# One transformer layer on one core: all q, k and v projected in a stage of their own before attention

## The chip, the cores and the metric

The kernel runs on one core of one Trainium2 chip. The metric is device time in microseconds for one execution of the whole layer; three runs of the kernel before gave a median of 2404.73 us (2404.29 to 2406.45). The engines are named as in the profile: PE is TensorE, DVE is VectorE, ACT is ScalarE, POOL is GpSimd, SP is SyncE, which here only issues DMAs.

## The reference

The sequence has 2048 tokens of width 1024, 16 heads of 64, and a feed-forward width of 2816. DEPTH is 1, so only layer 0 runs, and its mixer is the chunked softmax attention with a relative-position bias.

```python
def rms_norm(x, g):
    y = xf * lax.rsqrt(jnp.mean(xf * xf, axis=-1, keepdims=True) + RMS_EPS)
    return (y * g).astype(x.dtype)

def chunk_relpos_attention(h, w_qkv, w_o, rel_bias):      # CHUNK = 64, LEFT_CHUNKS = 8
    q, k, v = split_heads(h, w_qkv)
    for c in range(n_chunks):                             # chunk c reads chunks c-8 .. c
        sc = einsum(q_blk, k[:, :, k0:k1]) * scale + bias
        p = softmax(sc)
        outs.append(einsum(p, v[:, :, k0:k1]))
    return merge_heads(o) @ w_o

def reference(...):
    h = rms_norm(x, g_pre_mix);  m = chunk_relpos_attention(h, w_qkv, w_o, rel_bias)
    x = x + rms_norm(m, g_post_mix)
    h = rms_norm(x, g_pre_ffn)
    x = x + rms_norm((silu(h @ w_gate) * (h @ w_up)) @ w_down, g_post_ffn)
```

## The kernel before, in words

**Layout and products.** Activations lie transposed: 128 features on the partitions, tokens along the free axis, 512 tokens ("half", in the changed kernel "quarter", tiles of 128x512) at a time. Every float32 operand of a dense product is cut into a rounded part `hi` and a remainder `lo` (ACT makes `hi`, DVE subtracts to get `lo`: `split`, `split_part`), and a product is three PE matmuls, hi·hi, hi·lo and lo·hi (`products`, lines 207 to 209).

**Order of the work.** The PE order is the order in which the code issues it; the order on the other engines is set by a list scheduler when the kernel is built. Two groups of 1024 tokens are worked on one after the other. In a group, the attention of 16 jobs (8 pairs of heads times 2 halves) is the frame, and a generator `dense()` gives out the q, k, v and output projections in small pieces that `fill(t)` puts between the attention's steps. One job has four slots, one for each 128 queries. A slot issues: `scores` (q·k for two heads into the PSUM tile `st`, of which there is one; then on DVE the bias and the running minimum, one operation per head, on ACT the exponential, on DVE a reciprocal of the row sum, on POOL the scaling), dense filler, `transposed` (PE transposes of an earlier slot's probabilities into one of two PSUM tiles `tt`, four key blocks of each head, which DVE copies for the first head and ACT for the second; after more filler, the fifth key block of both heads), and once in a job `output` (probabilities times v into `po`). A job of the first 512 tokens has no earlier keys, so its slots have 128, 256, 384 and 512 keys instead of 640, and no fifth block.

**The filler.** `qk_job` makes one pair's q and k for one half from eight feature blocks, 2·8 products; `v_job` makes v for four heads with two matmuls for each feature block, of 512 and 256 columns (lines 540 and 543). Where a tile has to be laid out anew across partitions (`stage` to `q` and `k`), a DMA does it. `o_half` is the output projection of a half. The feed-forward part after it, of gate and up (`gate_up`) and down (`down`), uses seven block products in place of eight (`BLOCKS`: B11, B21, T1, T2, B22, T3, T4), with sums of blocks of the activations (class `Blocks`: `first`, `second`, `third`) and of the weights (S1 to S4). The weight sums are made in DRAM by accumulating DMAs that POOL issues (`weight_sums`), in the slots of the attention.

**The step from attention to feed-forward.** In the last group both calls of `o_half` stand behind the attention's end; `blocks[0].first` and `blocks[0].second`, which load x1, normalise it, form the sums and split them, run beside the two of them (lines 1440 and 1442).

Of the kernel before, what the change touches and what calls it, by code (L numbers as in the profile page):

```python
# [26 lines left out]
NG = SEQ // GROUP  # L27
NF = DFF // P
# [13 lines left out]
REST = 52  # L42

# [4 lines left out]
C256 = 0.110  # L48
QK_COST = 2 * KT * 3 * C512
V_COST = 4 * KT * 3 * C256  # L50


@with_exitstack
def trunk(
# [4 lines left out]
    w_a: bass.AP,  # L59
# [34 lines left out]
    attn_d = [[dram.tile([P, HALF], F32, name=f"attn_{p}_{i}") for p in range(NPAIR)] for i in range(2 * NG)]  # L94
    khist_d = [[dram.tile([P, 2, HALF], F32, name=f"kh_{p}_{g}") for p in range(NPAIR)] for g in range(NG - 1)]
    vhist_d = [[dram.tile([P, 4, 256], F32, name=f"vh_{j}_{g}") for j in range(NPAIR // 2)] for g in range(NG - 1)]
# [3 lines left out]
    sum_gu = {n: dram.tile([NF // 2, P, 1024], F32, name=f"gu_{n}") for n in ("S1", "S2", "S3", "S4")}  # L100
# [6 lines left out]
    def bias_rows():  # L107
        ext = phase["ap"].tile([P, 6 * HALF], F32, tag="k", name="ext", bufs=2)[0:NH, 0:EXT]
# [9 lines left out]
    plan, roomy = [], set()  # L118
    for g in range(NG):
        plan += [w_a[n] for n in range(3 * NPAIR // 2)]  # L120
        plan += [w_o[c] for c in range(4)] * 2
        if g == 0:
            roomy |= set(range(len(plan) - 6, len(plan) + 2))
# [17 lines left out]
    def fetch():  # L141
# [4 lines left out]
        raw = None  # L146
        if n in roomy:

            raw = phase["ap"].tile([P, 4 * HALF], F32, tag="q", name=f"raw_{n}", bufs=2)
            sp.dma_start(raw, plan[n])  # L150
        for c in range(2):
            here = slice(c * 1024, c * 1024 + 1024)
            if n in roomy:
                part = raw[:, here]
            else:
                if "fp" in phase:
                    part = phase["fp"].tile([P, 1024], F32, tag="w4", name=f"raw_{n}_{c}", bufs=4)
                else:
                    part = wp.tile([P, 1024], F32, tag="raw", name=f"raw_{n}_{c}", bufs=2)
                sp.dma_start(part, plan[n][:, here])  # L160
            split_part(*tiles[c], part)
# [4 lines left out]
    class Slab:  # L166
# [15 lines left out]
        def both(self, k):  # L182

            n = (k % 4) * 256
            return self.tiles[k // 4].both[:, :, n : n + 256]

# [10 lines left out]
    def dense_bank(n, wide=False):  # L197

        if "psf" in phase and n % 2:
            return phase["psf"].tile([P, HALF], F32, tag="pd", name="mm", bufs=6)  # L200
        if wide and n % 2:
            return phase["psa"].tile([P, 4, P], F32, tag="tt", name="mm", bufs=2).rearrange("p a b -> p (a b)")
        return ps.tile([P, HALF], F32, tag="mm", name="mm")
# [44 lines left out]
    def scratch(name):  # L248
# [6 lines left out]
        return xp.tile([P, 640], F32, tag="sc", name=name, bufs=4)  # L255
# [104 lines left out]
    class Prep:  # L360


        def __init__(self, s, src, gain):
            self.s, self.src, self.gain = s, src, gain
            self.done = set()

        def buffer(self):
            t = xp.tile([P, 10 * HALF], F32, tag="big", name="prep", bufs=1)
            self.t = t.rearrange("p (k c) -> p k c", k=10)
            self.total, self.r = self.t[:, 8, :], self.t[:, 9, :]  # L370

        def load(self, w=1.6, lag=3):

            def one(k):
                def go():
                    if k == 0:
                        self.buffer()
                    if k < KT:
                        sp.dma_start(self.t[:, k, :], self.src[:, k, :])
# [341 lines left out]
    def gather(g, s):  # L721
# [5 lines left out]
        for _ in range(2):  # L727
            yield
# [975 lines left out]
```

## Time and profile before

| | |
|---|---|
| median of three runs | 2404.73 us |
| span of the profiled execution | 2403.1 us |
| PE / DVE / ACT / POOL busy | 99% / 63% / 43% / 12% of the span |
| granted TensorE clock | 0.998 of full speed |
| DMA | 488.36 MB, mean 203 GB/s |

The profiled execution has a span, from its first to its last instruction, of 2403.1 us, 1.6 us under the median of the runs; the page gives no other time for it. Busy is time in which an engine had an instruction in hand; matmuls overlap in the pipeline, so a mean duration of a matmul (389 ns for 512 columns) is longer than the distance between two of them.

### The profile page before, as it was taken

The numbers are of one execution on the slowest core, as the hardware profiler recorded it, in microseconds if no ns is written. First come the engines' busy times: TensorE is split into PE (matmuls) and PEld (weight loads), VectorE is DVE, ScalarE is ACT, GpSimd is POOL, SyncE is SP. The second block draws the span as 40 slices with busy tenths as digits, with TensorE's granted clock in tenths as the row PEclk, the third lists the DMA queues.
The fourth block names the chain that finished last, engine by engine and source line by source line (L and its number), as shares of the span: only waits on it lengthen the run. The fifth ranks groups of instructions, "written<-read, shape, count | busy, mean of one in ns | idle before, by whom it ended". The sixth has DMA issues, their size and how long they took to land.

```text
span 2403.1 us, 33951 instructions
## 1 busy us (share of the span) xinstructions
PE 2381.4 (99%) x12054; PEld 1959.1 (82%) x12054; DVE 1524.6 (63%) x2690; ACT 1037.2 (43%) x1827; POOL 287.1 (12%) x376
## 2 busy tenths in 40 slices
PE   9999999999999999999999999999999999999998
PEld 8888888788787878778888888888888888888886
DVE  6555566587465555666677676677667765555577
ACT  6344444554344444545333343365443333334444
POOL 0233332102233322210000000000000000000002
PEclk9999999999999999999999999999999999999999
DMA  7688998657988875555576754577667654457664
GB/s 221 182 219 235 263 236 220 229 180 206 227 241 232 222 181 129 158 175 197 164 248 200 254 184 150 170 227 257 214 216 244 208 195 153 146 174 234 193 194 151
DMA packets 195833, 488.36 MB, mean 203 GB/s; under 512 B 25392, under 2 KB 27456, under 8 KB 185936
## 3 DMA queue, kind: packets, MB, share of 16 engines
q1 hardware_dynamic: 190032, 451.59, 58.7%
q0 software_dynamic: 5632, 34.61, 8.6%
q8 instruction: 95, 1.56, 0.3%
q14 instruction: 74, 0.61, 0.1%
HBM read 356.54 MB, written 148.42 MB: 210 GB/s over the span
## 4 chain that ended last, share of the span: by engine, by line
PE 56%; DVE 0%; DMA 0%; issue 0%; ACT 0%; POOL 0%; DVEq 0%; ACTq 0%
PE pd L207 6%; PE pd L208 6%; PE pd L209 6%; PE pb L208 5%; PE pb L209 5%; PE pb L207 5%; PE pc L208 3%; PE pc L209 3%; PE pc L207 3%; PE pa L207 3%; PE pa L209 3%; PE pa L208 3%; PE mm L207 1%; PE mm L209 1%; PE mm L208 1%; PE po L708 0%
## 5 line engine op out<-in xcount | busy, mean ns | idle before, releaser
L659 ACT ACTIVATE sc<-sc,nmax 128x640 f32<-128x640 f32 (+4 forms) x256 | 193.1, 756 | 235.8 <-DVE nmax L655 235.4
L207 PE MATMUL mm<-hb,w 128*128 128x512 f32 x704 | 283.7, 403 | 0.5 <-ACT y L268 0.5
L209 PE MATMUL mm<-hb,w 128*128 128x512 f32 x704 | 276.3, 392 | 0.0
L208 PE MATMUL mm<-hb,w 128*128 128x512 f32 x704 | 275.4, 391 | 0.0
L663 POOL TENSOR_SCALAR sc<-sc,rows 128x640 f32<-128x640 f32 (+4 forms) x256 | 192.5, 755 | 644.6 <-DVE rows L662 589.1
L655 DVE CUSTOM_DVE_ANT_0 sc<-st,bias 128x640 f32<-128x640 f32 (+4 forms) x256 | 179.4, 738 | 63.0 <-PE st L647 60.1
L207 PE MATMUL pb<-hb,w_gu_T 128*128 128x512 f32 x528 | 205.4, 389 | 0.0
L209 PE MATMUL pb<-hb,w_gu_T 128*128 128x512 f32 x528 | 205.4, 389 | 0.0
L208 PE MATMUL pb<-hb,w_gu_T 128*128 128x512 f32 x528 | 205.4, 389 | 0.0
L297 POOL TENSOR_TENSOR rs<-ms,neg_half 128x4 f32<-128x4 f32 (+1 forms) x7 | 10.5, 1496 | 1396.4 <-DVE ms L295 1396.4
L540 PE MATMUL mm<-w,hb 128*128 128x512 f32 x448 | 158.1, 396 | 0.0
L209 PEld LDWEIGHTS mm<-hb,w 128*128 128x128 f32 x704 | 132.1, 188 | 28.9
L207 PEld LDWEIGHTS mm<-hb,w 128*128 128x128 f32 x704 | 132.4, 188 | 24.5 <-issue 1.6
L208 PEld LDWEIGHTS mm<-hb,w 128*128 128x128 f32 x704 | 132.6, 188 | 22.3
L207 PE MATMUL pd<-a,w_d_T 128*128 128x512 f32 (+1 forms) x368 | 140.3, 381 | 0.2 <-ACT a L430 0.2
L208 PE MATMUL pd<-a,w_d_T 128*128 128x512 f32 (+1 forms) x368 | 139.9, 380 | 0.4 <-DVE a L431 0.4
L209 PE MATMUL pd<-a,w_d_T 128*128 128x512 f32 (+1 forms) x368 | 139.8, 380 | 0.0
L646 PE MATMUL st<-k,q 128*128 128x384 f32 (+1 forms) x448 | 137.9, 329 | 0.0
L207 PE MATMUL pa<-hb,w_gu_B 128*128 128x512 f32 x352 | 137.1, 389 | 0.5 <-ACT terms L1088 0.5
L209 PE MATMUL pa<-hb,w_gu_B 128*128 128x512 f32 x352 | 136.9, 389 | 0.0
L208 PE MATMUL pa<-hb,w_gu_B 128*128 128x512 f32 x352 | 136.9, 389 | 0.0
L679 PEld LDWEIGHTS tt<-ident,sc 128*128 128x128 f32 x928 | 106.8, 141 | 30.4 <-issue 18.1
(251 smaller groups left out, 5474.7 us busy)
## 6 DMA issues: line engine op xcount, KB each, us to landing
raw<-gu_S SPq DMA_DIRECT2D x88, 512.0 KB, 3.7
raw<-in_w_gu SPq DMA_DIRECT2D x66, 512.0 KB, 4.0
q<-stage SPq DMA_DIRECT2D x128, 256.0 KB, 6.1
y<-y SPq DMA_DIRECT2D x96, 256.0 KB, 3.8
gu_S<-in_w_gu SPq DMA_DIRECT2D x44, 512.0 KB, 6.4
raw_d<-d_S SPq DMA_DIRECT2D x88, 256.0 KB, 3.6
raw_a<-aT SPq DMA_DIRECT2D x88, 256.0 KB, 3.6
raw<-in_w_a SPq DMA_DIRECT2D x42, 512.0 KB, 6.7
```

Source lines behind the costliest of these rows:

```text
L207: pe.matmul(pt, a_hi, b_hi, start=first, stop=False, skip_group_check=go_on)
L208: pe.matmul(pt, a_hi, b_lo, start=False, stop=False, skip_group_check=go_on)
L209: pe.matmul(pt, a_lo, b_hi, start=False, stop=last, skip_group_check=go_on)
L297: pool.tensor_tensor(r[0][:, :nb], m[:, :nb], neg_half.to_broadcast([P, nb]), op=ALU.pow)
L540: both = lambda: pe.matmul(pt, ht.hi(k, c), w.both(k), start=k == 0, stop=k == KT - 1)
L646: pe.matmul(st[:, a:b], q[:, 2 * h, cols], kk[:, h, key], start=True, stop=False)
L655: dve.tensor_tensor_reduce(out=sc[:, :n], in0=st[:, c0 : c0 + n], in1=rev, scale=-1.0, scalar=3.0e38, op0=ALU.add, op1=ALU.min, accum_out= ...
L659: act.activation(sc[:, :n], sc[:, :n], AF.Exp, bias=nmax, scale=-1.0, accum_out=rows[:, 0:1])
L663: last_pool[0] = pool.tensor_scalar(sc[:, :n], sc[:, :n], rows[:, 1:2], 1.0, op0=ALU.mult, op1=ALU.mult)
L679: pe.transpose(tt[:, u, :], sc[h][:, b * P : b * P + P], ident)
```

## The change

**What it does.** (1) A new stage `project()` runs before any attention. It makes v for all tokens with three 512-column matmuls for each feature block (`values_of`), and q and k for all tokens with the seven block products that the feed-forward part already used (`queries_keys`, with `Blocks` over the normalised input and `block_items` for the weights). All of q, k and v go to DRAM (`emit_qk`, `emit_v`). (2) The attention works on quarters of 512 tokens, 8 jobs each, and loads q, k, v and bias for each job from DRAM (`Attend.load`). Its filler is the output projection of the quarter before (`o_quarter`), so the first quarter has none. Scores run two slots ahead of the transposes in place of one, the fifth block is copied by ACT, and the probabilities have six tiles of their own. (3) The last quarter's output projection stands alone behind the attention, with `blocks[0].first` and `.second` both beside it. (4) The weight sums of q/k and of gate/up are made by POOL in SBUF, four additions of 128x1024 for each unit of seven products; those of the down projection stay DMAs and are issued during `project()`. (5) `Blocks.first` has two of its four subtractions on POOL, `Late.write` its addition in the third and fourth quarter of attention.

**PE in the first quarter of the attention.** `st` are scores, `tt` transposes, `po` probabilities times v, `mm` a dense product. Before, from one slot of the first half:

```order
L646 MATMUL st<-k_1_855,q_0_1_786 128x512
L647 MATMUL st<-k_1_855,q_0_1_786 128x512
L646 MATMUL st<-k_1_855,q_0_1_786 128x512
L647 MATMUL st<-k_1_855,q_0_1_786 128x512
L207 MATMUL mm<-hb_4_183,w_1_699 128x512
L208 MATMUL mm<-hb_4_183,w_1_699 128x512
L209 MATMUL mm<-hb_4_183,w_1_699 128x512
L540 MATMUL mm<-w_0_1042,hb_1_178 128x512
L543 MATMUL mm<-w_0_1042,hb_1_178 128x256 x2
```

and of the change, from the same part of a job:

```order
L517 MATMUL tt<-ident,sc 128x128 x2
L484 MATMUL st<-k_1_4384,q_1_4381 128x512
L485 MATMUL st<-k_1_4384,q_1_4381 128x512
L484 MATMUL st<-k_1_4384,q_1_4381 128x512
L485 MATMUL st<-k_1_4384,q_1_4381 128x512
L517 MATMUL tt<-ident,sc 128x128 x4
L484 MATMUL st<-k_2_4500,q_2_4497 128x128
L485 MATMUL st<-k_2_4500,q_2_4497 128x128
L484 MATMUL st<-k_2_4500,q_2_4497 128x128
L485 MATMUL st<-k_2_4500,q_2_4497 128x128
```

Between two writes of the one tile `st` there were dense products; now only transposes stand there.

**PE in a slot of the last quarter.** Before, from the transposes on:

```order
L679 MATMUL tt<-ident,sc 128x128 x8
L207 MATMUL py<-hb_13_9971,w_0_9742 128x512
L208 MATMUL py<-hb_13_9971,w_0_9742 128x512
L209 MATMUL py<-hb_13_9971,w_0_9742 128x512
L207 MATMUL py<-hb_13_9971,w_0_9742 128x512
L208 MATMUL py<-hb_13_9971,w_0_9742 128x512
L209 MATMUL py<-hb_13_9971,w_0_9742 128x512
L207 MATMUL py<-hb_13_9971,w_0_9742 128x512
L208 MATMUL py<-hb_13_9971,w_0_9742 128x512
L209 MATMUL py<-hb_13_9971,w_0_9742 128x512
L690 MATMUL tt<-ident,sc 128x128 x2
```

and of the change:

```order
L517 MATMUL tt<-ident,sc 128x128 x8
L184 MATMUL mm<-hb_25_5737,w_0_8223 128x512
L185 MATMUL mm<-hb_25_5737,w_0_8223 128x512
L186 MATMUL mm<-hb_25_5737,w_0_8223 128x512
L528 MATMUL tt<-ident,sc 128x128 x2
```

The same transposes, with three matmuls of filler between those of four blocks and those of the fifth, where nine stood. Of the 96 slots of the later quarters, 32 have one product (three matmuls) on either side of the eight transposes, 30 have two on one side and one on the other, and 15 go from the eight transposes straight to the fifth block behind `po`.

**DVE in the same slots of the change.** `sc,nmax<-st,bias` is the operation on the scores of one head, `pT<-tt` the copy of the first head's four transposed blocks:

```order
L493 ISA sc,nmax<-st,bias_4386 128x640
L493 ISA nmax 128x1
L493 ISA sc,nmax<-st,bias_4391 128x640
L493 ISA nmax 128x1
L520 COPY pT<-tt 128x4x128
L500 RECIPROCAL rows<-rows 128x1 x2
```

The copy, for which the fifth block's transposes on PE wait (there are two tiles `tt`), is behind both operations on the scores that PE has issued last.

**The diff, cut to its core.**

```diff
-    def qk_job(g, s, p, w):
-                products(pt, w.hi(k, c), w.lo(k, c), ht.hi(k), ht.lo(k), k == 0, k == KT - 1)
+    def emit_qk(n, p, which, src):
+        act.activation(hi, src, AF.Copy, scale=scale)
+        dve.scalar_tensor_tensor(lo, src, scale, hi.bitcast(F32), op0=ALU.mult, op1=ALU.subtract)
+        for a, part in enumerate((hi, lo)):
+            part = part.bitcast(F32)
+            if which == 0:
+                sp.dma_start(q_d[n][p][:, a, :], part)
+                continue
+            for h, own in enumerate(heads):
+                sp.dma_start(k_d[n][p][heads[a], h, :], part[own])
...
+        def load(self):
+            for half in heads:
+                sp.dma_start(self.q[half].rearrange("d (h a) c -> d h (a c)", h=2).bitcast(F32), src)
+            if self.prev:
+                sp.dma_start(self.kk[:, :, 0:HALF].bitcast(F32), k_d[n - 1][p])
+            sp.dma_start(self.kk[:, :, HALF:].bitcast(F32), k_d[n][p])
+            self.bias = [bias_tile(NH * n + 2 * p + h, 2 * p + h) for h in range(2)]
...
-                dve.tensor_copy(self.pT[:, :, 4, cols], tt[:, 0:2, :])
+                act.activation(self.pT[:, :, 4, cols], tt[:, 0:2, :], AF.Copy)
...
+    def block_items(w_, c):
+        def make(n):
+            w = w_tile(f"w{c}_{n}")
+            split_part(*w, r[FACTOR[n]])
+            if n == "B21":
+                raw("S1")
+                r["S2"], r["S3"], r["S4"] = r["A11"], r["A21"], r["A12"]
+                for to, a, b in (("S1", "A21", "A22"), ("S3", "A21", "A11"), ("S2", "A11", "S1"), ("S4", "A12", "S2")):
+                    last_pool[0] = pool.tensor_tensor(r[to], r[a], r[b], op=ALU.add)
+            return w
...
+    def values_of(n, cols, between):
+                for m in range(4):
+                    products(pts[m], cols.hi(k, c), cols.lo(k, c), hi, lo, k == 0, k == KT - 1)
...
+    def project():
...
+        for g in range(NG):
+            later.extend(scaled(a, totals[a], 4.0) + scaled(b, totals[b], 4.0) + group.first(1.5))
+            yield from values_of(a, held[a], None)
+            later.extend(group.second(2.2))
+            yield from values_of(b, held[b], None)
+            later.extend(group.third(1.0))
+            yield from queries_keys(g, group, after)
...
+    for t in range(-2, slots):
+        if t + 2 < slots:
+            job.scores((t + 2) % 4)
+        share = (0.4 if t % 4 == 0 else 1.2) * left[0] / max(per - t % per - 1, 1)
+        fill(0.45 * share)
+        if t > 0 and t % 4 == 0:
+            jobs[t // 4 - 1].output()
+            if t % per == 0:
+                work, left[0] = o_quarter(n), KT * KT * 3 * C512
+        if t >= 0:
+            jobs[t // 4].transposed(t % 4, lambda: fill(0.55 * share))
...
+    later.extend(blocks[0].spreads() + pause(1.0) + blocks[0].first(1.2) + blocks[0].second(1.6))
+    for c in o_quarter(NQ - 1):
+        tick(c / (3 * C512))
```

More of the change, by code (lines that the diff above doesn't have):

```diff
@@ L1462, in dense @@
                 later.extend(blocks[0].third(1.5) + pause(44.0))
[L1463 to L1465 removed]
+                late = lates[NQ - 1]
+                later.extend(late.rows(1.5) + late.write(8.5))
                 later.extend(pause(12.0) + blocks[1].sums(7.0, True))
```

855 lines of the change are left out of this document (298 added, 557 removed).

## The prediction

> **What bounds the kernel now.** I read the page's busy line first, then what PE waited for, then the busy time by stretches of 100 us, and last the timeline of one attention slot.
>
> ```profile
> span 2403.1 us, 33951 instructions
> ...
> PE 2381.4 (99%) x12054; PEld 1959.1 (82%) x12054; DVE 1524.6 (63%) x2690; ACT 1037.2 (43%) x1827; POOL 287.1 (12%) x376
> ```
> ```profile
> PE tt L690 <- DVE pT L682: 1.8, 4, 0.8
> ```
> ```profile
> 1200.00:1300.00 100.00, 100.00 (x443) 82.81 (x442) 74.32 (x102) 36.95 (x50) 0.00 (x0) 1.00 0.72 233
> ```
>
> PE has work in hand for 99% of the span, and the longest entry in its list of waits is 1.8 us in total. In the feed-forward part 443 matmuls of 512 columns start in 100 us, so one costs 100/443 = 0.2257 us. The time before is thus a count of matmuls, and any wait that the change makes on PE adds in full.
>
> ```profile
> 693.96 0.42 PE L646 MATMUL st<-k,q 128*128 128x384 f32 x1
> ...
> 695.04 0.34 PE L647 MATMUL st<-k,q 128*128 128x384 f32 x1
> 695.21 0.28 PE L543 MATMUL mm<-w,hb 128*128 128x256 f32 x1
> ...
> 695.52 0.82 DVE L655 CUSTOM_DVE_ANT_0 sc<-st,bias 128x640 f32<-128x640 f32 x1 [0.68 <-PE st L647]
> 695.56 0.28 PE L543 MATMUL mm<-w,hb 128*128 128x256 f32 x1
> ...
> 696.27 0.82 DVE L655 CUSTOM_DVE_ANT_0 sc<-st,bias 128x640 f32<-128x640 f32 x1
> ...
> 697.02 0.08 DVE L655 DVE_READ_ACCUMULATOR2_ANT nmax<- 128x1 f32 x1
> 697.07 4.53 PE L708 MATMUL po<-pT,v 128*64 128x512 f32 x32
> ...
> 701.52 1.09 PE L679 MATMUL tt<-ident,sc 128*128 128x128 f32 x8
> ...
> 702.37 0.36 PE L543 MATMUL mm<-w,hb 128*128 128x256 f32 x1
> ```
>
> In this slot the scores take PE from 693.96 to 695.21; DVE begins on them at 695.52 and is done at 697.10, 1.9 us after PE left them. Eight transposes take 702.37 - 701.52 = 0.85 us. Before, dense products cover those 1.9 us and all that follows from them.
>
> **What the change saves.** q and k: 4 halves x 8 pairs x 2 x 8 x 3 = 1536 matmuls become 2 groups x 4 units x 7 products x 24 = 1344; 192 x 0.2257 = 43.3 us less. v: one feature block of 512 + 256 columns took 695.56 - 695.21 = 0.35 us, 512 of them 179.2 us; after, 768 matmuls take 173.3: 5.9 us less. Output projection, feed-forward part and the attention's own matmuls are the same in number. With no new wait the span would be 2403.1 - 49.2 = 2353.9 us.
>
> **What it adds on PE.** Everything moved off PE's way is hidden only while DVE, ACT, POOL or a DMA stays ahead of PE. I go through the places in order of time.
>
> *Projection.* While PE makes the first v of a group (192 x 0.2257 = 43.3 us), DVE has 8 `lo` columns, 16 weight splits and `Blocks.first`, and the last come bunched. By the rows quoted below for the step to the feed-forward part that is 8 x 0.75 + 16 x 0.69 + 25.8 = 43 us. Between 0 (the weights are split three products ahead) and 15 us over both groups, I take 4.
>
> *From projection to attention.* The first job's loads are in SP's queue behind the last `emit_qk`, hence behind two DVE operations and one ACT operation (about 2 us after PE's last product), then a transfer:
>
> ```profile
> q<-stage SPq DMA_DIRECT2D x128, 256.0 KB, 6.1
> ...
> k<-kh SPq DMA_DIRECT2D x8, 512.0 KB, 7.5
> ```
>
> 2 + 7.5 gives 10 us with PE idle; bounds 8 (the 6.1 row) and 14.
>
> *First quarter, 8 jobs, no filler.* DVE and PE per job:
>
> ```profile
> L655 DVE CUSTOM_DVE_ANT_0 sc<-st,bias 128x512 f32<-128x512 f32 x16 | 10.4, 687 | 4.5 <-PE st L647 4.5
> L655 DVE CUSTOM_DVE_ANT_0 sc<-st,bias 128x384 f32<-128x384 f32 x16 | 8.4, 555 | 9.8 <-PE st L647 9.6
> L655 DVE CUSTOM_DVE_ANT_0 sc<-st,bias 128x256 f32<-128x256 f32 x16 | 6.1, 421 | 2.3 <-PE st L647 2.3
> L655 DVE CUSTOM_DVE_ANT_0 sc<-st,bias 128x128 f32<-128x128 f32 x16 | 4.1, 286 | 0.7 <-PE st L647 0.3
> ...
> L662 DVE RECIPROCAL rows<-rows 128x1 f32<-128x1 f32 x256 | 39.8, 159 | 41.6 <-ACT sc L659 40.5
> ...
> L682 DVE COPY pT<-tt 128x512 f32<-128x512 f32 x104 | 71.1, 684 | 19.8 <-PE tt L679 18.4
> L682 DVE COPY pT<-tt 128x384 f32<-128x384 f32 x8 | 4.3, 542 | 0.0
> L682 DVE COPY pT<-tt 128x256 f32<-128x256 f32 x8 | 3.3, 418 | 0.7 <-PE tt L679 0.5
> L682 DVE COPY pT<-tt 128x128 f32<-128x128 f32 x8 | 2.3, 283 | 0.4 <-PE tt L679 0.4
> ...
> L431 DVE TENSOR_TENSOR hb<-po,hb 128x512 fp32r<-128x512 f32 x4 | 2.8, 689 | 8.9 <-ACT hb L430 8.9
> ```
> ```profile
> 85.00 2.38 PE L708 MATMUL po<-pT,v 128*64 128x512 f32 x16
> 87.31 1.09 PE L679 MATMUL tt<-ident,sc 128*128 128x128 f32 x8
> ```
>
> DVE: 2 x (0.687 + 0.555 + 0.421 + 0.286) + 8 x 0.08 + 8 x 0.159 + (0.684 + 0.542 + 0.418 + 0.283) + 0.689 = 8.4 us. PE: 5120 score columns 2.3, 20 transposes 2.1, `po` 2.3, together 6.7 us. DVE is therefore the bound, at 8 x 1.7 = 14 us lost or more. Its order also puts reciprocals, which wait for an exponential just begun, ahead of the next operation on `st`, and PE cannot write `st` until that is done. Laid out by hand, a job comes to between 9 and 11 us; I take 9.9, so 8 x 3.2 = 26 us (14 to 36). Loads of 2.3 MB in 9.9 us are no bound: 235 GB/s stands against
>
> ```profile
> 693.00:712.00 19.00, 19.00 (x128) 15.16 (x127) 8.88 (x23) 7.11 (x16) 5.16 (x7) 1.00 0.96 294
> ```
>
> *Later quarters.* With one product either side of the eight transposes, PE asks for the second use of a `tt` tile 0.68 + 0.85 + 0.68 = 2.2 us after the scores; the copy that frees it comes behind both operations on the scores, at 1.9 + 0.68 = 2.6. That is 0.4 us in 32 slots, 12.8 us. In 15 slots the fifth block follows straight on the eight transposes, and the row of waits gives 1.8/4 = 0.45 for that, 6.8 us. In some 18 slots a weight split or a row sum stands ahead of the copy; at 0.2 us shown for each, 3.6. Sum 23 us, from 5 (DVE's order in time better than as listed) to 40 (those 18 show in full).
>
> *From attention to feed-forward.* `first` and `second` now share one output projection of 43.3 us.
>
> ```profile
> L866 DVE SCALAR_TENSOR_TENSOR b<-b,gt,row 128x512 f32<-128x512 f32 x36 | 26.1, 751 | 9.7 <-DMA b<-x 9.0 <-ACT row L352 0.7
> ...
> L431 DVE TENSOR_TENSOR hb<-b,hb 128x512 fp32r<-128x512 f32 x44 | 29.7, 689 | 0.7 <-ACT hb L430 0.6
> ...
> L139 DVE TENSOR_TENSOR w<-raw,w 128x1024 fp32r<-128x1024 f32 x78 | 97.8, 1255 | 31.7 <-ACT w L138 31.2
> ```
> ```profile
> 1070.00:1080.00 10.00, 10.00 (x46) 8.26 (x45) 10.00 (x16) 4.95 (x7) 0.00 (x0) 1.00 0.92 311
> ```
>
> DVE was already full there with 87 us of PE beside it. `first` has 16 x 0.751 + 20 x 0.69 = 25.8 us (norms; two sums and three splits for each k), `second` 8 x 1.44 = 11.5, eight weight splits 10, seven row sums 4.8: 52 us, of which four norms and splits of B22 (5.8) are due only four products later. 46 against 43.3, and some 4 us until the first loads land: 6 us, from 0 to 14.
>
> *Weight sums on POOL.*
>
> ```profile
> L1516 POOL TENSOR_TENSOR hb<-hb,hb 128x512 f32<-128x512 f32 x3 | 4.2, 1417 | 4.3 <-ACT sq L272 3.0 <-DVE hb L1515 1.3
> ...
> L472 DVE SCALAR_TENSOR_TENSOR hb<-hb,gt,total 128x512 f32<-128x512 f32 x8 | 8.8, 1135 | 0.0
> ...
> L1283 DVE SCALAR_TENSOR_TENSOR y<-y,gt,total 128x512 f32<-128x512 f32 x32 | 23.7, 750 | 17.3 <-DMA y<-y 14.8 <-DMA out_dram<-y 2.2
> ```
>
> No addition of 128x1024 is in the trace; twice 1.417 is 2.8 us, four 11.3, in a unit of 168 x 0.2257 = 37.9. The third, S2, is asked for two products (10.8 us) after the first can start and is ready after 8.5. I put 2 us on it, between a gain of 2 (no accumulating DMAs in the attention) and a loss of 30 (second rival).
>
> **The sum.** 2353.9 + 4 + 10 + 26 + 23 + 6 + 2 = 2424.9 us of span. The median before lies 1.6 above the span, so I predict 2426 us, 0.9% slower. 0.2% is about what a measurement here can tell from no change: 2400 to 2410.
>
> **Rivals.**
> *VectorE keeps pace in the attention.* If, in the attention, only DVE's busy time binds (14 us in the first quarter) and the copies come before PE asks (0), 35 us go: 2391, faster. For it: DVE is busy 47% in the slot's stretch quoted above. Against: the listed order. It decides below 23 us of waits in the attention, in place of 49.
>
> *POOL's sums slow DVE.* L472 took 1135 ns beside a POOL addition against 750 alone. DVE has some 28 us of work in a unit; lengthened by half in POOL's 11 to 17 us it still fits 37.9, but evacuations come late. At 1 us in each of 30 units: 2456. [...]
>
> *The PE clock falls in the first quarter.*
>
> ```profile
> 2388.00:2392.00 4.00, 3.06 (x27) 2.90 (x26) 3.79 (x8) 2.44 (x6) 1.33 (x1) 1.00 0.00 0
> 2392.00:2396.00 4.00, 0.69 (x5) 0.36 (x4) 3.42 (x7) 0.00 (x0) 2.10 (x2) 0.76 0.58 199
> 2396.00:2400.00 4.00, 0.00 (x0) 0.00 (x0) 3.01 (x5) 0.00 (x0) 1.85 (x2) 0.50 0.61 206
> ```
>
> The granted clock was 1.00 while PE was busy 3.06 of 4 us and 0.50 some microseconds after it stopped. If it stays at 0.50 through the first quarter, a job's 6.7 us become 13.4, 8 x 3.5 = 28 us on top: 2454. Against: PE would be busy some 70% there. [...]
>
> **How the numbers follow.** Main case 0.50, its own range 2405 to 2450; VectorE keeps pace 0.27; POOL 0.13; clock 0.10. Most of the 0.27 lies under 2400, the rest with the main case's lower end inside 0.2%: faster 0.27, same 0.13, slower 0.60. Range: from the low ends of both attention terms with the others as taken (2426 - 12 - 18 = 2396, and less where the projection and the step cost nothing, 2382) to the POOL or the clock case with a part of another, 2466.
>
> **What would show it.** Of the profile after: PE idle about 10 us where `st` first appears; jobs of the first quarter 9 to 11 us apart, PE waiting there for DVE's operation on `st`; the line of the fifth block's transposes waiting for `pT` copies, near 23 us in all; no wait on POOL in the attention; a clock of 1.00 in the first quarter; DVE full in the last output projection. I am wrong if PE's waits in the attention sum to under 23 us, or if waits appear inside the units of seven products.

## The result and the profile after

The changed kernel takes 2571.56 us, median of four runs (2567.99 to 2576.70), against 2405.59 for the kernel before on the same chip: a ratio of 1.0693, 95% interval 1.0678 to 1.0708. The prediction was 2426 us, at most 2466. Slower was right, and the size was wrong: the change costs 166 us, not 21.

The page of the profiled execution (span 2574.6 us) shows it in its first lines, engine busy times:

```profile
span 2574.6 us, 33484 instructions
...
PE 2405.3 (93%) x11562; PEld 1942.4 (75%) x11562; DVE 1715.4 (67%) x2679; ACT 1156.4 (45%) x2047; POOL 648.8 (25%) x501
```

PE has 492 matmuls fewer and is busy 24 us longer, and it is idle for 169 us in place of 22. DVE is busy 191 us longer with fewer instructions. The same execution, cut at the steps of the work (columns: from and to; length, busy time of PE, PEld, DVE, ACT, POOL; granted clock, DMA share, GB/s). The rows are the first v, the first q and k, the second v, the second q and k, the step to the attention, its first quarter, its other quarters, the last output projection, and the feed-forward part:

```profile
0.00:121.00 121.00, 103.39 (x425) 83.36 (x426) 91.53 (x120) 65.15 (x110) 38.30 (x27) 0.92 0.63 211
121.00:282.00 161.00, 154.78 (x675) 127.78 (x674) 116.81 (x129) 75.00 (x112) 36.78 (x15) 0.98 0.61 184
282.00:389.00 107.00, 95.46 (x409) 77.13 (x408) 68.35 (x97) 45.50 (x76) 28.82 (x24) 0.94 0.78 245
389.00:559.00 170.00, 159.82 (x674) 130.18 (x673) 94.61 (x100) 56.20 (x78) 60.33 (x49) 0.96 0.78 222
559.00:572.50 13.50, 0.15 (x1) 0.00 (x0) 1.38 (x2) 0.63 (x1) 0.58 (x4) 0.61 0.83 213
572.50:682.40 109.90, 81.68 (x459) 62.23 (x459) 66.30 (x258) 64.96 (x188) 40.09 (x72) 0.87 0.95 233
682.40:1187.80 505.40, 476.06 (x3031) 361.27 (x3031) 307.08 (x750) 308.09 (x671) 177.53 (x204) 0.99 0.75 211
1187.80:1255.50 67.70, 53.24 (x241) 41.72 (x241) 54.29 (x69) 31.85 (x51) 24.71 (x12) 0.90 0.60 202
1255.50:2574.60 1319.10, 1280.73 (x5657) 1058.78 (x5655) 915.05 (x1159) 509.01 (x767) 241.72 (x98) 0.98 0.50 164
```

There is no one place: every stage has idle PE time, and nearly every one a clock below 1.00, where before the mean was 0.998. Summed over stretches of 5 us, PE's busy time multiplied by what the clock lacked comes to 51 us of matmul time lost to the clock. That is a count, not a saving: where PE has to wait anyway, a faster matmul may only wait longer. What PE waited for, longest totals first (total, times, longest):

```profile
PE st L484 <- DVE nmax L493: 24.4, 22, 2.1
PE tt L528 <- DVE pT L520: 18.0, 29, 2.0
PE pb L184 <- DVE terms L890: 17.5, 6, 5.6
PE pb L184 <- DVE terms L1156: 15.7, 4, 6.2
PE pv L185 <- DVE w_v L131: 14.9, 5, 7.0
PE st L484 <- DMA k<-k: 13.4, 1, 13.4
PE mm L186 <- DVE w L131: 10.4, 2, 9.5
PE tt L528 <- ACT pT L522: 7.1, 6, 1.5
```

The attention is where I looked for them. But four of these eight lie outside it: a block product that waits for DVE to empty its PSUM tile (L890, L1156), and a product that waits for a weight split (`w_v`, `w`). One of them from near, in the second q, k stage (start, length; in brackets the idle time ahead and its releaser):

```profile
503.96 11.29 POOL L810 TENSOR_TENSOR raw<-raw,raw 128x1024 f32<-128x1024 f32 x4 [7.46 <-DMA raw<-in_w_qk]
504.19 2.72 DVE L426 SCALAR_TENSOR_TENSOR lo<-terms,hi 128x512 fp32r<-128x512 f32 x1 [0.70 <-ACT hi L425]
506.82 0.68 DVE L1156 TENSOR_TENSOR terms<-pc,terms 128x512 f32<-128x512 f32 x1
507.43 2.82 DVE L131 TENSOR_TENSOR w_w_B<-raw,w_w_B 128x1024 fp32r<-128x1024 f32 x1
...
510.17 2.84 DVE L426 SCALAR_TENSOR_TENSOR lo<-terms,hi 128x512 fp32r<-128x512 f32 x1
512.94 0.68 DVE L1156 TENSOR_TENSOR terms<-pb,terms 128x512 f32<-128x512 f32 x1
...
513.76 0.47 PE L184 MATMUL pb<-hb,w_w_T 128*128 128x512 f32 x1 [2.84 <-DVE terms L1156]
```

POOL makes four weight sums in a row. Each of the three DVE operations that read two SBUF tiles (L426, L131) outlasts the POOL addition that was under way when it began, ending 0.55 to 0.56 us (L426) and 1.08 us (L131) after it, and takes 2.7 to 2.8 us; where no weight sum overlaps, these lines take 0.69 and 1.22 in the mean. The operations between them, with one operand in PSUM, take their 0.68. The evacuation for which PE waits is behind three such operations and comes 2.84 us late. By groups, in all of the changed kernel (busy time, mean ns):

```profile
L886 DVE TENSOR_TENSOR terms<-terms 128x512 f32<-128x512 f32 x42 | 67.4, 1604 | 30.6 <-ACT terms L871 30.6
L890 DVE TENSOR_TENSOR terms<-pb,terms 128x512 f32<-128x512 f32 x86 | 58.4, 685 | 36.1 <-PE pb L186 36.1
L810 POOL TENSOR_TENSOR raw<-raw,raw 128x1024 f32<-128x1024 f32 x120 | 318.8, 2656 | 1001.0 <-DVE w_w_T L131 328.0 <-DVE y L985 252.3 <-DVE w_w_B L131 157.3
```

L886 and L890 are the same operation on the same size. L886, with both operands in SBUF, takes 2.3 times as long in the mean: 29 of its 42 overlap a weight sum in time (mean 2016 ns), 13 do not (686). Of the operations of L890 with `pb` or `pc`, which have one operand in PSUM, 55 overlap a weight sum, and none took more than 692 ns.

### The profile page after: what moved, and what is told of

Same layout as the page of the kernel before. It is cut to its first block, busy times and chain, and to the rows that moved or that the text cites. A ratio compares the mean times of both kernels' runs of the same rounds, so it can differ in the third digit from the quotient of the medians.

```text
span 2574.6 us, 33484 instructions
## 1 busy us (share of the span) xinstructions
PE 2405.3 (93%) x11562; PEld 1942.4 (75%) x11562; DVE 1715.4 (67%) x2679; ACT 1156.4 (45%) x2047; POOL 648.8 (25%) x501
## 5 line engine op out<-in xcount | busy, mean ns | idle before, releaser
L810 POOL TENSOR_TENSOR raw<-raw,raw 128x1024 f32<-128x1024 f32 x120 | 318.8, 2656 | 1001.0 <-DVE w_w_T L131 328.0
L184 PE MATMUL pb<-hb,w_w_T 128*128 128x512 f32 x720 | 287.6, 400 | 33.3 <-DVE terms L890 17.5
L186 PE MATMUL pb<-hb,w_w_T 128*128 128x512 f32 x720 | 285.8, 397 | 0.0
L185 PE MATMUL pb<-hb,w_w_T 128*128 128x512 f32 x720 | 285.6, 397 | 0.0
L184 PE MATMUL pa<-hb,w_w_B 128*128 128x512 f32 x480 | 189.2, 394 | 5.2 <-ACT terms L871 4.5
L184 PEld LDWEIGHTS pb<-hb,w_w_T 128*128 128x128 f32 x720 | 138.8, 193 | 66.9 <-issue 23.6
L185 PE MATMUL pa<-hb,w_w_B 128*128 128x512 f32 x480 | 188.6, 393 | 0.0
L186 PE MATMUL pa<-hb,w_w_B 128*128 128x512 f32 x480 | 188.2, 392 | 0.0
L484 PE MATMUL st<-k,q 128*128 128x384 f32 (+1 forms) x448 | 146.3, 346 | 38.2 <-DVE nmax L493 24.4
L131 DVE TENSOR_TENSOR w_w_T<-raw,w_w_T 128x1024 fp32r<-128x1024 f32 x120 | 163.4, 1362 | 22.5 <-ACT w_w_T L130 21.9
L131 DVE TENSOR_TENSOR w_w_B<-raw,w_w_B 128x1024 fp32r<-128x1024 f32 x90 | 116.1, 1290 | 89.0 <-ACT w_w_B L130 88.9
L130 ACT ACTIVATE w_w_T<-raw 128x1024 fp32r<-128x1024 f32 x120 | 126.7, 1056 | 98.1 <-PE pa L186 43.7
L185 PEld LDWEIGHTS pb<-hb,w_w_T 128*128 128x128 f32 x720 | 139.1, 193 | 28.9
L186 PEld LDWEIGHTS pb<-hb,w_w_T 128*128 128x128 f32 x720 | 138.4, 192 | 29.6
L130 ACT ACTIVATE w_w_B<-raw 128x1024 fp32r<-128x1024 f32 x90 | 95.2, 1058 | 125.2 <-PE pb L186 82.3
L892 ACT ACTIVATE terms<-terms 128x512 f32<-128x512 f32 x65 | 41.1, 632 | 210.5 <-DVE terms L890 210.5
```

Source lines behind the costliest of these rows:

```text
L130: act.activation(hi, raw, AF.Copy)
L131: dve.tensor_tensor(lo, raw, hi.bitcast(F32), op=ALU.subtract)
L184: pe.matmul(pt, a_hi, b_hi, start=first, stop=False, skip_group_check=go_on)
L185: pe.matmul(pt, a_hi, b_lo, start=False, stop=False, skip_group_check=go_on)
L186: pe.matmul(pt, a_lo, b_hi, start=False, stop=last, skip_group_check=go_on)
L484: pe.matmul(st[:, a:b], q[:, 2 * h, cols], kk[:, h, key], start=True, stop=False)
```

## The experiments

All times are medians of four runs (two for the last), the kernel before being at 2405.7 to 2406.6 us beside them. An interval is that of the ratio to the kernel before.

### Whose is POOL's part: four runs

**`no_sums`**: the weight sums left out.

```diff
-                    last_pool[0] = pool.tensor_tensor(r[to], r[a], r[b], op=ALU.add)
+                r["S1"], r["S2"], r["S3"], r["S4"] = r["A22"], r["A11"], r["A21"], r["A12"]
```

> Leaves out the 120 additions of weight blocks on POOL (the sums are replaced by plain blocks, so the output is not the reference's). Exclusion theory (a POOL operation holds up every DVE operation that reads two SBUF tiles until it ends): the gate-up products of two SBUF tiles fall from a mean of 1604 ns to about 690, PE's waits inside the units of seven products go (4.84, 1.78, 2.84 in q and k, 4.72, 3.81, 4.46, 1.06, 1.51, 4.50, 5.58, 1.09 in gate and up, part of 5.56 in the first v: some 40 us), and with them eight stretches at a granted clock of 0.5 that cost 3.4 us each: 2571.6 - 67 = 2505 (2490 to 2520). Rival (DVE simply has too much work in a bunch, POOL matters little): at most 15 us less, 2557 or more.

**`sums_dve`**: the same sums on DVE.

```diff
-                    last_pool[0] = pool.tensor_tensor(r[to], r[a], r[b], op=ALU.add)
+                    dve.tensor_tensor(r[to], r[a], r[b], op=ALU.add)
```

> The same 120 additions of weight blocks on DVE in place of POOL. Exclusion theory: DVE gets 120 x 1.25 = 150 us more, but no operation of 2.66 us beside it; from the time without the additions up to 20 us above it, 2505 to 2525. Rival (DVE's amount of work is what counts): the units get 5 us more of DVE each, slower than the changed kernel, 2575 to 2600.

**`sub_dve`**: the two subtractions of `Blocks.first`, the additions of `Late.write` and the square sums of the second token block (a `columns` call with `dve` for `pool`) back on DVE. One of the lines:

```diff
-                pool.tensor_tensor(t3, b12, b22, op=ALU.subtract)
+                dve.tensor_tensor(t3, b12, b22, op=ALU.subtract)
```

> The two subtractions of Blocks.first, the addition of Late.write and the square sums of the second token block are back on DVE; the additions of weight blocks stay on POOL. Exclusion theory: PE's waits in the v stages and in the last output projection (2.69, 1.86, 6.96, 3.31, 9.54 us, with four half-clock stretches of 3.4: 38 us) lose about half, since a subtraction on POOL held DVE up for about 1.05 us where it would have taken 0.68 there, and DVE also waited 1.17 for its result: 2550 (2535 to 2565). Rival (amount of work on DVE): 24 x 0.69 = 16 us more of DVE in the fullest places, 2572 to 2585.

**`no_pool`**: both of the last two edits.

> Both: no addition or subtraction of two SBUF tiles is left on POOL but in the very last steps. Exclusion theory: the gains add, 2485 (2465 to 2510); what is left above 2355 is then the first quarter, the copies, the transition, the bunched norms and the clock after those. Rival (amount of work on DVE): 2575 or more.

Measured: 2528.03 (1.0503, 1.0485 to 1.0521), 2533.36 (1.0532, 1.0516 to 1.0547), 2574.33 (1.0697, 1.0679 to 1.0715) and 2525.94 (1.0496, 1.0471 to 1.0521). POOL's weight sums cost 44 us; on DVE they cost 5, within the intervals, though DVE then spends 146 us on them. The group of `sums_dve` that stood at 1604 ns:

```profile
L886 DVE TENSOR_TENSOR terms<-terms 128x512 f32<-128x512 f32 x42 | 28.8, 687 | 11.9 <-ACT terms L871 11.9
L810 DVE TENSOR_TENSOR raw<-raw,raw 128x1024 f32<-128x1024 f32 x120 | 146.4, 1220 | 12.0 <-DMA raw<-in_w_gu 8.4 <-DMA raw<-in_w_qk 2.3
```

One addition takes DVE 1220 ns and POOL 2656. On POOL it took no work from DVE: DVE is busy for 1715 us with the sums on POOL and for 1715 with the sums on DVE, against 1586 without them. The amount of DVE's time therefore does not make the 38 us between the two kernels; where in its queue the time falls, and when the sums are ready, can. The feed-forward part of `no_sums` (1240.9 to its end), against the last row of the table by stage:

```profile
1240.90:2520.20 1279.30, 1266.88 (x5657) 1050.43 (x5655) 824.02 (x1158) 510.12 (x767) 17.69 (x12) 1.00 0.51 168
```

The same 5657 matmuls take 39.8 us less, at a clock of 1.00. (The profiled executions lie 5 us above the median in the changed kernel and 6 below it in `no_sums`, so their spans differ by 54 us where the medians differ by 44.)

All of this agrees with the exclusion theory, but there is a second effect beside it that no run here separates: POOL needs 11.3 us for four additions where DVE needs 4.9 (4 x 1.22), so the sums are ready later. In the changed kernel ACT, which splits them, waits for POOL's sums for 28.0 us in 16 waits, and PE once waits behind ACT:

```profile
1920.67 1.06 ACT L130 ACTIVATE w_w_T<-raw 128x1024 fp32r<-128x1024 f32 x1 [5.02 <-POOL raw L810]
1921.64 1.06 ACT L871 ACTIVATE terms<-pa 128x512 f32<-128x512 f32 x2
...
1922.27 0.79 PE L184 MATMUL pa<-hb,w_w_B 128*128 128x512 f32 x1 [4.50 <-ACT terms L871]
```

That the sums on POOL cost 44 us is shown; how much of it is blocked DVE operations and how much late sums is not.

`no_sums` gained less than the 67 us that I expected: in it PE waits 8.5 and 8.2 us in the second v, where DVE's order came out otherwise. From `sub_dve` I expected 22 us and got none; the subtractions may be as dear on POOL, by blocking, as on DVE, but POOL's weight sums were still there. In `no_pool` the gains were to add, to 2485 us (2465 to 2510); it stays at 2526, 7 us below `sums_dve` with intervals that overlap. Its rival, 2575 or more, is out all the same.

### The first quarter: three runs

`two_st` and `busy_pe` start from `no_pool`, as do the two runs of the next part.

**`two_st`**: in the first quarter, the scores of every second slot go to two other PSUM banks.

```diff
+            if not self.prev and ib % 2:
+                two = [ps.tile([P, HALF], F32, tag="mm", name="st") for _ in range(2)]
```

> Beside the run with no POOL additions (2525.9): in the first quarter the scores of every second slot go to two further PSUM banks, so PE can write the next scores while DVE is on the last. Theory (one tile for the scores: PE waits for DVE's operation on it, 24.6 us in 22 waits): jobs of the first quarter come 8.7 us apart in place of 11.3, and the half-clock stretches there (8.6 us) go: 2501 (2494 to 2512). Rival (the chain of one slot through DVE, ACT and POOL to the transposes sets the pace): jobs stay 11 us apart, 2520 to 2530.

Measured: 2525.23 (1.0488, 1.0471 to 1.0505), no change. But the wait went: on `nmax` 5.9 us are left of 24.6, and another has come (PE's waits in `two_st`, then 60 us of its first quarter):

```profile
PE st L489 <- DMA k<-k: 24.7, 7, 13.7
```
```profile
580.00:640.00 60.00, 47.89 (x274) 36.13 (x274) 35.71 (x150) 35.26 (x110) 22.36 (x42) 0.86 1.03 232
```

The DMA engines are busy without a gap, and jobs stay some 11 us apart on the mean. The theory was right on the wait that one sees, and a second bound lay right behind it.

**`two_st_no_bias`**: from `two_st`, without the bias loads of the first quarter from its third job on.

```diff
+        if 4 <= n < NH:
+            return t
```

> Beside the run with two tiles for the scores (2525.2): the first quarter's jobs after the second load no bias (the output is not the reference's), 0.58 MB of 2.37 MB for a job. Theory (with the tile for the scores doubled, the loads of 2.37 MB at some 235 GB/s set the 11 us of a job): a job takes 1.79 MB / 235 = 7.6 us of DMA, so DVE's 8.4 us bind, jobs come 8.5 to 9.2 us apart: 2525 - 8 x 2 - half-clock stretches of 6 = 2503 (2497 to 2512). Rival (the chain of a slot through DVE, ACT and POOL sets it, the DMAs only fill the time): jobs stay 11 us apart, 2520 to 2530.

Measured: 2510.27 (1.0428, 1.0411 to 1.0445). The same 60 us:

```profile
580.00:640.00 60.00, 51.49 (x342) 40.20 (x338) 45.14 (x177) 42.79 (x130) 28.23 (x50) 1.00 0.88 224
```

Jobs are 8.6 to 9.2 us apart (by the start of `po`), the quarter takes 94.6 us in place of 108.6, and the clock is 1.00 in this stretch. The rival, a chain through DVE, ACT and POOL, is thereby out. So two bounds stand at 11 us: the one tile of the scores, and loads of 2.37 MB a job at 220 to 232 GB/s (580 to 640 us in `no_pool` and in `two_st`). Fewer loads with the one tile, which would show the first bound by itself, was not run.

**`busy_pe`**: idle matmuls during the first load (26) and one ahead of the scores of each slot of the first quarter.

```diff
+        pe.matmul(idle[:, 0:P], ident, ident, start=True, stop=True)
```

> Beside the run with no POOL additions (2525.9): idle matmuls of 128 columns that nobody reads, 26 of them while PE waits for the first loads of the attention and one ahead of the scores of each slot of the first quarter. Clock theory (PE's waits halve the granted clock for some 7 us): the granted clock stays near 1.00 there, the half-clock loss of 8.6 us in the first quarter goes, while at most a few us of the added matmuls show: 2518 (2512 to 2523). Rival (PE's clock does not count there, since DVE sets the pace): 2526 to 2541, the 31 added matmuls of 0.47 us showing in part.

Measured: 2529.25 (1.0510, 1.0495 to 1.0526). No gain, as the rival has it, and it tells little: the 26 lasted 6.0 us, PE was then idle for another 7.67, and the first score matmul of 128 columns took 0.45 us, like 0.44 at that place in the changed kernel, where the clock was at 0.50, and unlike 0.33 there at 606.69, where it was at 1.00.

### Filler and weight sums by DMA: two runs

**`fill_late`**: the filler behind the transposes.

```diff
-        fill(0.45 * share)
+        fill(0.1 * share)
...
-            jobs[t // 4].transposed(t % 4, lambda: fill(0.55 * share))
+            jobs[t // 4].transposed(t % 4, lambda: fill(0.9 * share))
```

> Beside the run with no POOL additions (2525.9): of the output projection's filler a tenth stands ahead of the eight transposes and nine tenths behind them, in place of 45 and 55 hundredths. Theory (PE asks for the fifth block's tile before its copy is made): of the 25.9 us that PE waits there some 16 go, 2509 (2502 to 2516). Rival (DVE's order is late whatever stands on PE; the waits move to the scores' tile): 2522 to 2530.

Measured: 2511.06 (1.0436, 1.0421 to 1.0452), 15 us less, as expected. PE's waits for the fifth block in `fill_late` are 12 us in all, from 25.8 in `no_pool` and 25.1 in the changed kernel:

```profile
PE tt L528 <- ACT pT L522: 7.0, 4, 2.5
PE tt L528 <- DVE pT L520: 5.0, 14, 0.4
```

**`late_sums`**: the accumulating DMAs of the down projection in the second quarter of the attention.

```diff
-        if done > 400.0 and done % 4.0 < 1.0:
-            next(sums_, None)
...
+        if t >= per:
+            next(sums_, None)
```

> Beside the run with no POOL additions (2525.9): the accumulating DMAs for the weight sums of the down projection are issued in the second quarter of the attention, not in the second half of the projection. Theory (they fill the DMA engines, stores of q and k are late, DVE waits for the tiles they leave): PE's wait of 3.06 us in the second q, k stage and some 2 us of half clock go, and the transition gets shorter by 2 us: 2519 (2514 to 2524). Rival (bunched DVE work makes those waits): 2523 to 2529; if the attention's loads suffer in turn, above that.

Measured: 2541.69 (1.0561, 1.0543 to 1.0578). The second q, k stage with the transition does shorten, by 5.6 us. The attention's loads then come late, as the last clause of the rival has it:

```profile
PE st L484 <- DMA k<-k: 31.6, 7, 13.3
```

13.3 of it is the first load; the other 18, with the clock lost (0.96 from 650 to 1180 us, for 0.99 in `no_pool` from 660 to 1165), lengthen the later quarters by 28 us. The change's early place for these DMAs is the better one.

### Bunched work: two runs

**`paced`** (from `fill_late`): the steps of `first`, `second`, `third` and `columns` given out more slowly.

```diff
...
-    later.extend(blocks[0].spreads() + pause(1.0) + blocks[0].first(1.2) + blocks[0].second(1.6))
+    later.extend(blocks[0].spreads() + pause(1.0) + blocks[0].first(2.6) + blocks[0].second(3.2))
```

> Beside the run with the filler behind the transposes (2511.1): the same work, but the steps that load, normalise, sum and split the activations for the next stage are given out more slowly: first at 2.6 and 4.0 products a step in place of 1.5, second 6.0 in place of 2.2, third 3.0 for 1.0, the columns of the second group 2.8 for 1.6, and beside the last output projection 2.6 and 3.2 for 1.2 and 1.6. Theory (DVE has the work bunched in the first half of a stage, and weight splits and evacuations queue behind it): PE's waits of 3.8, 4.5, 6.6, 3.6 and 8.4 us go for the most part, with the half-clock stretches after them: 2480 (2472 to 2492). Rival (DVE's sum of work in these stages is the limit, however it is laid out): 2503 to 2520.

Measured: 2497.75 (1.0390, 1.0366 to 1.0414), 13 us less, between the theory's range and the rival's. From the end of the last `po` to the first block product PE takes 46.3 us in place of 58.4, and waits there for 0.8 us in all, as expected. But the feed-forward part gets 15 us longer; at its start:

```profile
1205.74 0.15 DVE L272 TENSOR_SCALAR ms<-pssq 128x4 f32<-128x4 f32 x1
...
1205.98 3.19 POOL L274 TENSOR_TENSOR rs<-ms,neg_half 128x4 f32<-128x4 f32 x1 [59.66 <-DVE ms L272]
...
1209.22 1.12 PE L334 MATMUL prs<-ident,rs 128*128 128x128 f32 x4 [15.08 <-POOL rs L274]
```

An operation of 0.15 us for the square roots stood behind 14 us of DVE work, and PE with it.

**`paced_roots`** (from `paced`): ten to fourteen products between the two PE steps of a root, and `third` ahead of it; `first`, `third` and `columns` also get a somewhat denser spacing again. Cut to the projection's roots:

```diff
-            later.extend(scaled(a, totals[a], 4.0) + scaled(b, totals[b], 4.0) + group.first((2.6, 4.0)[g]))
+            sa, sb = scaled(a, totals[a], 0.0), scaled(b, totals[b], 0.0)
+            later.extend(pause(5.0) + [sa[0], sb[0]] + pause(10.0) + sa[-2:] + sb[-2:] + group.first((2.0, 3.0)[g]))
```

> Beside the paced run (2497.8): the square-root chains (sums on PE, a small DVE and a POOL operation, then four transposes on PE) get 10 to 14 products between their first and their last PE step, both token blocks of a group together, and stand behind `third` at the start of the feed-forward part; the columns of the second group come at 2.4 products a step, first at 2.0 and 3.0. Theory (the waits of 6.4, 9.4 and 15.1 us on a sum or a root are what the bunched work turned into: the small DVE operation stands behind the large ones): they fall to a few us with their half-clock stretches, 2468 (2458 to 2480). Rival (DVE has too much to do around the step and the projection, the wait moves again): 2490 to 2505.

Measured: 2489.33 (1.0346, 1.0324 to 1.0367). The 15 us wait is gone. Two on the sum ahead of a root stay:

```profile
PE pssq L267 <- DVE total L250: 14.0, 2, 8.8
```

So both theories hold in part, and this time is at the rival's edge. The bunching is real (22 us for the two edits), and around the v stages a wait moved rather than went, as the rival says; whether DVE's amount of work is the limit there, these runs do not show. This is the fastest version that I found, still 3.5% behind the kernel before; whether another could beat it stays open.

### What a wait does to the clock: three runs

**`pe_kept_on`** (from `fill_late`) and **`paced_kept_on`** (from `paced_roots`): 44 and 80 idle matmuls ahead of the first scores, with the line shown under `busy_pe`.

> Beside the run with the filler behind the transposes (2511.1): 44 idle matmuls of 128 columns (0.31 us each by the run with 26 of them) that nobody reads, while PE waits 13.3 us for the first loads of the attention; none elsewhere. Clock theory (the wait itself halves the granted clock for some 7 us): the first 20 us of the first quarter are at a granted clock of 1.00 in place of 0.50 to 0.57, and the quarter ends some 3 us sooner, 2508 (2504 to 2512). Rival (the matmuls of the first slots are waited for by nobody): the clock is 1.00 there, and the quarter ends no sooner, 2509 to 2514.

> Beside the run before it in this list: 80 idle matmuls of 128 columns (0.227 us each by the run with 44) ahead of the first scores, so that PE is busy for all of its wait for the first loads. Clock theory: the granted clock is 1.00 over the first 20 us of the first quarter in place of 0.50, and the time from the first scores to the first `po` falls from about 18 us to 14; in all 0 to 4 us less, since up to 5 us of the matmuls may stick out behind the loads. Rival (the clock falls there for another reason): 0.50 in that stretch all the same, and no shorter.

Measured: 2518.30 (1.0466, 1.0451 to 1.0482) and 2494.50 (1.0368, 1.0351 to 1.0385), 7 and 5 us above their bases, the 5 within the intervals. With 44, PE was still idle for 6.63 us, so the first tells nothing. With 80 the clock was held, for a while (`paced_kept_on`):

```profile
545.00:550.00 5.00, 3.83 (x33) 3.48 (x31) 1.22 (x9) 0.88 (x4) 0.55 (x2) 1.00 1.09 241
550.00:555.00 5.00, 3.86 (x13) 2.88 (x14) 2.42 (x14) 2.56 (x9) 2.30 (x5) 0.62 1.03 237
555.00:560.00 5.00, 3.06 (x14) 2.29 (x12) 2.96 (x13) 2.63 (x8) 1.58 (x3) 0.50 0.98 210
```

It fell a few us later, with the scores begun: to 0.62 and 0.50 in rows where PE was busy for 3.86 and 3.06 of 5 us. From the first scores to the first `po` it took 15.5 us, against 17.2 without the idle matmuls, but they stuck out behind the loads: PE's step to the attention grew from 12.9 to 17.6 us. Keeping PE busy through the load bought nothing.

**`pauses`**: in the kernel before, a pause of PE ahead of each of nine units.

```diff
+            pe.matmul(a, ident, ident, start=True, stop=True)
+            act.activation(t, a, AF.Copy)
+            for _ in range(n):
+                act.activation(t, t, AF.Copy)
+            pe.matmul(b_, t, ident, start=True, stop=True)
```

> The kernel before, with a pause of PE ahead of each of nine units of the first gate-up stage: a matmul whose operand a chain of 1, 3, 5, 8, 11, 14, 18, 25 and 37 ACT copies of 128x128 makes (output unchanged; pauses of about 1 to 11 us). Clock theory: pauses up to about 3 us cost their own length; after longer ones the matmuls come 0.43 us apart for some 6.8 us, which costs 3.4 us more, whatever the length: 45 to 55 us of pauses and five to six times 3.4, 2405 + 70 = 2475 (2460 to 2490). Rival (a pause costs its own length and no more): 2450 to 2460, with the granted clock at 1.00.

Measured: 2476.43 (1.0293, 1.0272 to 1.0314). Four of the nine pauses in its timeline, and the stretch after the second of these, by 1 us:

```profile
1244.84 0.49 PE L1087 MATMUL hold<-ident,held 128*128 128x128 f32 x2 [2.50 <-ACT held L1086]
...
1287.24 0.49 PE L1087 MATMUL hold<-ident,held 128*128 128x128 f32 x2 [3.58 <-ACT held L1086]
...
1378.48 0.79 PE L1087 MATMUL hold<-ident,held 128*128 128x128 f32 x2 [5.58 <-ACT held L1086]
...
1481.42 0.80 PE L1087 MATMUL hold<-ident,held 128*128 128x128 f32 x2 [12.78 <-ACT held L1086]
```
```profile
1287.00:1288.00 1.00, 0.76 (x4) 0.72 (x5) 0.37 (x1) 0.18 (x1) 0.00 (x0) 0.94 1.10 158
1288.00:1289.00 1.00, 1.00 (x3) 0.71 (x3) 0.00 (x0) 0.00 (x0) 0.00 (x0) 0.50 0.78 160
1289.00:1290.00 1.00, 1.00 (x4) 0.80 (x3) 0.00 (x0) 0.00 (x0) 0.00 (x0) 0.50 0.88 317
1290.00:1291.00 1.00, 1.00 (x4) 0.81 (x3) 0.00 (x0) 0.00 (x0) 0.00 (x0) 0.50 0.86 336
1291.00:1292.00 1.00, 1.00 (x5) 0.77 (x5) 0.00 (x0) 0.00 (x0) 0.00 (x0) 0.85 0.30 115
```

After pauses of 1.14, 1.37 and 2.50 us the clock stays at 1.00; after 3.58 and all longer ones (4.55, 5.58, 8.12, 12.78, 13.67) it falls to 0.50. That these waits of 3.58 to 13.67 us by themselves halved the clock is thereby shown, in a kernel with no other change. The price was over-sized: from pause to pause, less the unit and the next pause, PE takes 0.9 to 1.4 us where the clock held (the added matmuls among them) and 2.3 to 3.4 us after a fall: some 1 to 2.5 us beyond the pause's own length, not 3.4. That the time came out at 2476 for 2475 is luck in part: the pauses add up to 53 us and the added matmuls, which I had left out, to some 8.

## Why the prediction was wrong, point by point

I go by its own terms. The numbers for the changed kernel are idle time plus matmul time lost to the clock (both summed over stretches of 5 us) in that stage.

- **Saving, 49.2 us: right in work, 27 us in time.** PE's busy time less the clock's loss falls from 2381 to 2354. Most of the rest lies in the first quarter, where PE counts as busy, the clock's loss taken off, for 71 us for what I had counted as 8 x 6.7 = 54; why, no run shows.
- **Projection, 4 (0 to 15): measured about 63** (2.9 us idle at the start, as in the kernel before, taken off). This is the step that failed most. I set 43 us of DVE work against 43.3 of PE work and took the difference, as if the two ran side by side without a wait; but this work is queued in the first half of a stage, with the weight splits and evacuations behind it, and POOL's weight sums lengthen it. In the trace DVE is busy for 92 us of the first v, whose 384 matmuls cost 87. By the same count the projection has 42 us in `no_pool` and 35 in `paced_roots`, so the runs show some 21 us to be POOL's and 7 the spacing's. What makes the other 35, most of it in the two v stages, stays open; the waits there are for the sum ahead of a root and for weight splits.
- **Projection to attention, 10 (8 to 14): 13.4.** Inside the bounds. The transfer took the 7.5 us that I priced; the load of k was issued 5.9 us after PE's last product, where I had 2.
- **First quarter, 26 (14 to 36): 39,** of it 28 idle and the rest clock. DVE's order and the wait on `st` are as laid out, jobs 10.7 to 12.3 us apart for the 9.9 that I took. The sentence that the loads are no bound failed: the quoted 294 GB/s is not what these loads reach, and without the wait on `st` the DMA engines run full at 232 (`two_st`, share 1.03).
- **Later quarters, 23 (5 to 40): 25.1** for the two rows of the fifth block, with some 6 of clock and 3.7 of a first product beside them. Right in cause, and `fill_late` confirms it. That the size fits is luck in part: I had 65 slots of 0.2 to 0.45 us, all on DVE's copy, and the trace has 35 waits of 0.72 in the mean, 7.1 us of them on ACT's.
- **Attention to feed-forward, 6 (0 to 14): 16,** by the same bunching (9.5 us on one weight split). Behind it come 4.7 us for a root, whose small DVE operation stood behind three subtractions of 6.2 us in all beside a weight sum.
- **Weight sums on POOL, 2 (-2 to 30): 44.** The second failed step; part of these 44 lies in the projection and is in its 63 too. I had the row that speaks against it (1135 ns beside POOL against 750) and misread it: it is a mean of two kinds. In the trace of the kernel before, five of its eight operations take 0.74 to 0.75 us and the three that began while a POOL operation ran 1.78 to 1.79, which is 2.4 times and not half more. In the changed kernel's timeline above, operations of two SBUF operands take 2.72 to 2.84 us beside additions of 2.66 in the mean. Then I weighed DVE's mean load, where the place in the queue counts, and gave the case 0.13. The same row speaks against the two subtractions on POOL; I had taken them as DVE work saved.
- **The clock: no term at all.** I gave it to the first quarter alone, as a rival of 0.10. Measured, it costs 51 us over all stages, and each of PE's 14 waits of more than 3 us stands at a half-clock stretch (6.8 to 27.3 us long).
- **Rivals:** VectorE did not keep pace. The POOL rival came true and beyond its price (44 us for 30). Of the clock rival a part did: in the first quarter the clock is 0.87 and not 0.50, some 11 us for the 28, and the rest of its loss lies in other stages. I had treated both as exclusive of the main case, and let a range reach only to one of them "with a part of another". Of the two signs of being wrong that I named, the second came: waits inside the units of seven products, 33 us in ten (L890, L1156).

The sum now: 27 us saved, idle time up by 148, 51 us lost to the clock: 2403 - 27 + 148 + 51 = 2575, which holds by the way that the 27 are counted. Of the 166 us of medians, runs account for 46 (POOL), 15 (filler) and 22 (pacing and roots). The remaining 83, half of the miss, no edit that keeps the output took away. Where PE still loses time is seen in the trace of `paced_roots`: 42 us in the first quarter (idle 27.8, clock 14.2), 24 in the other quarters, 13 in the step to the attention, 32 in the two v stages.

## What to carry to other kernels

Where PE is 99% busy, a count of matmuls saved is a bound, not a forecast: price each wait by what stands ahead of the releasing operation in its engine's queue in that stage, not by the engine's mean load, and add 1 to 2.5 us for each wait of 3.58 us or more, which is what `pauses` showed (none for 2.50 or less). Work of two SBUF operands that was moved to POOL took nothing off DVE here, which ran such operations too (1715 us busy with the weight sums on either engine); on DVE itself it was cheaper (5 us for 44). When a wait is taken away, ask what stands right behind it: the first quarter had a second bound at 11 us behind the first, and removing the first moved nothing.

## What was not expected of the hardware

The half-clock stretches in `pauses` come in steps. Summed over rows of 1 us, the clock was at 0.50 for 3.42 and 3.40 us (pauses of 3.58 and 4.55), 6.84 and 6.82 (5.58 and 8.12), 13.66 and 13.64 (12.78 and 13.67): once, twice and four times 3.41. The six falls, read from the same rows, lie 44.4, 44.4, 47.8, 47.8 and 54.6 us apart, which is 13, 13, 14, 14 and 16 times 3.41. After a pause of 3.58 us the fall came when PE was at work again. And the clock also fell without a long wait: in the first quarter of the changed kernel from 580 to 660 us no wait passes 1.54 us, and the clock was at 0.50 for 3.42 us from 609.8, where PE had been busy for 2.39 of the 5 us before 610. In `no_pool` it is 0.66 from 610 to 615, where the five us before had PE busy for 2.78.

The second surprise is how a DVE operation's operands decide: beside a POOL addition in the changed kernel, a subtraction or addition on 128x512 took 0.68 to 0.69 us with one operand in PSUM (L890: 55 operations, mean 0.686, at most 0.692) and up to 2.89 with both in SBUF (L886: 29, mean 2.02).
